# Later residual loads in the down product, an eighth slot for input tiles, and the gate's columns in quarters of the tokens

## The chip, the cores and the metric

The kernel runs on one core of one Trainium2 chip. The metric is the device time of one execution in microseconds (us), median of the runs; lower is better. The engines that matter are TensorE (PE in the profile, its weight loads PEld), VectorE (DVE), ScalarE (ACT), GpSimd (POOL) and SyncE (SP), whose queue issues nearly all DMA transfers.

## The reference

One layer on 1024 tokens of width 1024, all in float32:

```python
h = _rmsnorm(x, mix_norm_gain[l])
proj = h @ w_in[l]                                   # 1024 -> 3232 columns
y_rwkv = _rwkv7_mixer(proj[..., :RWKV_COLS], ...)    # 8 heads, gated delta rule; gate columns gd
o = _dilated_attention(q, k, v)                      # 8 heads, three dilations
x = x + jnp.concatenate([y_rwkv, y_attn], axis=-1) @ w_out[l]
h = _rmsnorm(x, ffn_norm_gain[l])
gate, val = jnp.split(h @ w_ffn_up[l], 2, axis=-1)   # 2 x 2816 columns
gate = _causal_dwconv(gate, ffn_conv_w[l], ffn_conv_b[l])
x = x + (jax.nn.silu(gate) * val) @ w_ffn_down[l]    # 2816 -> 1024
return _rmsnorm(x, final_norm_gain)
```

## The kernel before, in words

Every large product is made of two halves per operand: an upper half (the value rounded to the matmul's format, names with `hi` or `h`) and a lower half (value minus upper half, `lo` or `l`). A product is three matmuls: upper by upper, lower by upper, upper by lower (lines 475 to 477, 1752 to 1754). So each tile that is loaded costs a cast for the upper half (mostly ScalarE) and a subtraction for the lower one (VectorE or GpSimd, `lower`, line 301).

Order is written out by a planner, `Plan`: each operation has the engines that may do it with a cost, a rank, and the operations it comes after. `run` takes the operation that can start first by these costs, and the lowest rank among equals. The result is a fixed list of instructions for each engine. An engine works its list in order: an instruction that waits holds back all that is behind it, on SP too. A slot of a ring (`ring(name, n, ...)`) is given to a new tile when the tile n places earlier has been read by all its users. The operations named in `after` order the plan alone; in the program an instruction waits for data and for memory.

**Start (lines 404 to 574).** Eight tiles of x (128 tokens each, `x_0` to `x_7`) are loaded, two for each of four turns. `norm_turn` squares each (ScalarE, line 370, scratch `jk_n`), takes the reciprocal root (GpSimd), scales the tile (VectorE, line 376), transposes it in eight pieces (TensorE, line 386, into `pt_n`), and writes the upper and lower half of the transposed input, `hT_hi` (line 292 or 294) and `hT_lo` (line 395). Then `in_proj` multiplies by column blocks of w_in: `wa` (64 columns, twice), `gd` (the gate's 96 columns), then `k`, `r`, `v` and the attention's. Each block sums 512 tokens in one bank (`pb_wa`, `pb_gd`), first tokens 0 to 511, then the others. With `cut=2` the first 512 tokens are worked in two quarters of 256, so that they can begin when two turns are done. The banks come from a ring of two, so the second half of `wa` waits until the first has been read (`zwa`, and `carry_wa`, line 504). Small loads follow the input: `cst2`, `lwr` and `glr`, whose casts are `lwh` and `gl`. `grow_d` (line 337) writes 1024 gains of `par` to DRAM as a row, for the second norm far later.

**Down product (lines 1671 to 1772).** The 2816 rows of w_down are 22 factors of 128. Factor f needs a tile of the activation (`ra`, loaded from `act_d`) and one of the weights (`rw`), each split into four halves by `operand`. The steps (`groups`) hold one factor, one, and then three each. In a step the sums `pd` of eight token tiles by two column halves are formed in a ring of six banks and added to `dx` (line 1760; the first step copies instead, line 286 or 288). `residual` loads the layer's input `x1_d` into `dxs` and adds it to `dx` (line 1697) in steps three to six; `final` does the last norm in the last step. The load of a residual has a rank of its own and depended on `x1_stored` alone.

Of the kernel before, what the change touches and what calls it, by code (L numbers as in the profile page):

```python
# [18 lines left out]
P = 128  # L19
S = 1024  # L20
D = 1024
KD = D // P
# [9 lines left out]
GCOLS = 96  # L32
# [172 lines left out]
def planned_layer(ctx: ExitStack, tc: tile.TileContext, a, out):  # L205
    nc = tc.nc
# [13 lines left out]
    def ring(tag, n, shape, pool, dtype=F32):  # L220
        plan.ring(tag, n)
        if pool.space == PSUM:
            plan.banks.add(tag)

        def new(name):
            return plan.buf(tag, lambda: pool.tile(shape, dtype, tag=tag, name=name, bufs=n))

        return new
# [49 lines left out]
    def pool(us):  # L278
        return {POOL: us}
# [4 lines left out]
    def copy(eng, out, in_):  # L284
        if eng == ACT:
            nc.scalar.copy(out, in_)
        else:
            nc.vector.tensor_copy(out, in_)  # L288
# [10 lines left out]
    def lower(eng, lo, t, hi):  # L299

        either_of(eng).tensor_tensor(lo, t, f32(hi), ALU.subtract)  # L301
# [25 lines left out]
    def derived():  # L327
# [6 lines left out]
    g_ = _off["ffng"]  # L334
    grow_out = plan.op(
        {SP: 0.5},
        lambda: nc.sync.dma_start(out=grow_d.rearrange("o (k p) -> p (o k)", p=P), in_=par[:, g_ : g_ + KD]), -150, [par_in],
        lag=1.0,
    )
    par_in = plan.op({DVE: 0.5}, derived, -270, [par_in])  # L340
# [76 lines left out]
    scmask, bones = pc_[:, 0:256], pc_[:, 256:384]  # L417
    h_in = []
    with tc.tile_pool(name="xp", bufs=1) as xp:
        x_n, jk_n = ring("x", 7, [P, D], xp), ring("xjk", 1, [P, D], xp)  # L420
        for g in range(4):
            src = []
            for i in (2 * g, 2 * g + 1):
# [14 lines left out]
        def in_proj(cols, name, R, evacuate, after=None, Rw=None, twice=False, cut=1):  # L438

            raw, hi, lo = w_n(f"wr_{name}"), h_n(f"wh_{name}"), wl_n(f"wl_{name}")
            at, ins, Rw = 0, [], R if Rw is None else Rw
            for c0, n in cols:
                ins.append(
                    load(
                        raw, lambda at=at, n=n: raw.t[:, :, at : at + n],
                        lambda c0=c0, n=n: w_in[:, c0 : c0 + n].rearrange("(k p) c -> p k c", p=P), 1.46 * max(n, 128) / P, Rw,
                        [chain.get("w")],
                    )  # L450
                )
                at += n
            r, m = at, at * (1 + twice)

            def wide():
                return raw.t[:, :, None, :r].broadcast_to([P, KD, 2, r]) if twice else raw.t[:, :, :r]

            def parted(t):
                return t[:, :, :m].rearrange("p k (x c) -> p k x c", c=r) if twice else t[:, :, :m]

            Rw = max(Rw, -279.5)
            o = chain["w"] = plan.op(COPY, lambda eng: copy(eng, parted(hi.t), wide()), Rw, ins, [raw, hi, lo])
            o2 = plan.op(
                pool(2.3), lambda: lower(POOL, parted(lo.t), wide(), parted(hi.t)), Rw, [o], [raw, hi, lo]
            )
            outs = []
            for n in range(2):
                acc = acc_n(f"pb_{name}_{n}")
                d, c = None, 1 if n else cut
                for q, k in product(range(c), range(KD)):  # L470
                    w = 512 // c
                    ts_, cs = slice(n * 512 + q * w, n * 512 + (q + 1) * w), slice(q * w, (q + 1) * w)

                    def step(k=k, acc=acc, ts_=ts_, cs=cs):
                        nc.tensor.matmul(acc.t[:m, cs], hi.t[:, k, :m], hT_hi[k][:, ts_], start=(k == 0), stop=False)  # L475
                        nc.tensor.matmul(acc.t[:m, cs], hi.t[:, k, :m], hT_lo[k][:, ts_], start=False, stop=False)  # L476
                        nc.tensor.matmul(acc.t[:m, cs], lo.t[:, k, :m], hT_hi[k][:, ts_], start=False, stop=(k == KD - 1))  # L477

                    quarters = range(ts_.start // 256, ts_.stop // 256)
                    d = plan.op(  # L480
                        pe(0.69 / c), step, R, [o, o2, d, after, *(x for g in quarters for x in h_in[g][k])], [hi, lo, acc]
                    )
                outs.append(evacuate(n, acc, m, d))
            return outs

        def shift_mix(sh, dst, R, name, bufs=()):

            carry = st.tile([P, 1], F32, name=f"carry_{name}", bufs=1)

            def evacuate(n, acc, m, d):  # L490
                mu = par[:m, _off["sh_r"] + sh : _off["sh_r"] + sh + 1]
                c0 = n * 512

                def shifted():
                    t = dst()
                    nc.vector.scalar_tensor_tensor(
                        t[:m, c0 + 1 : c0 + 512], acc.t[:m, 0:511], mu, t[:m, c0 + 1 : c0 + 512], ALU.mult, ALU.add
                    )
                    if n:
                        nc.vector.scalar_tensor_tensor(  # L500
                            t[:m, 512:513], carry[:m], mu, t[:m, 512:513], ALU.mult, ALU.add
                        )
                    else:
                        nc.vector.tensor_copy(carry[:m], acc.t[:m, 511:512])

                o = plan.op(
                    {ACT: 0.57, DVE: 0.66},
                    lambda eng: scaled(eng, dst()[:m, c0 : c0 + 512], acc.t[:m], omm[:m, sh : sh + 1]), R, [d, par_in],
                    [acc, *bufs],
                )  # L510
                return plan.op({DVE: 0.79}, shifted, R, [o], [acc, *bufs])

            return evacuate
# [27 lines left out]
        lw_in = plan.op(LOW, lambda eng: lower(eng, flat(lwl), lwr.t, flat(lwh)), -184, [o], [lwr])  # L541

        zg = tmp_n("zg")
        z_in = in_proj([(1600, GCOLS)], "gd", -198, shift_mix(13, lambda: zg.t, -198, "gd", [zg]), None, -288.5)
        gr = slice(0, GCOLS)
        xg = pa_.tile([P, 2, S], F32R, name="xg")
        gl = pa_.tile([P, 2, RW], F32R, name="gl")
# [1136 lines left out]
    def down(acts, early, dp, pacc):  # L1684
# [4 lines left out]
        acc_n = ring("dacc", 6, [P, 512], pacc)  # L1689
        xr = [xr_n(f"dx{i}") for i in range(8)]  # L1690
        xsum = {i: [[], []] for i in range(8)}

        def residual(i, R):
            xs = jk_n(f"dxs{i}")
            o = load(xs, lambda: xs.t, lambda: x1_d[i], 1.46, R - 2, [x1_stored[i]])
            o = plan.op(
                {DVE: 1.22}, lambda: nc.vector.tensor_add(xr[i].t, xr[i].t, xs.t), R, [o, *xsum[i][0], *xsum[i][1]], [xs, xr[i]]
            )
            xsum[i] = [[o], [o]]
# [37 lines left out]
        for gi, fs in enumerate(groups):  # L1737
            R = 601 + 2 * gi
            ops = [operand(f, R, acts, raw_n, [(dh_n, dl_n)] * 2) if f else early for f in fs]
            if gi == 1:  # L1740
                fg_in = plan.op({SP: 0.5}, lambda: nc.sync.dma_start(out=fg, in_=a["fgain"].broadcast_to([P, D])), 990, lag=1.5)
            for i in range(8):
                ts_ = slice((i % 4) * P, (i % 4) * P + P)
                for n in range(2):
                    sl = slice(n * 512, (n + 1) * 512)
                    pd = acc_n(f"pd{gi}_{i}_{n}")
                    d = None
                    for j, o4 in enumerate(ops):
                        (ah, al, a_in), (wh, wl, w_in_) = o4[i // 4], o4[2 + n]

                        def step(j=j, ah=ah, al=al, wh=wh, wl=wl, ts_=ts_, pd=pd, n_=len(ops)):
                            nc.tensor.matmul(pd.t, ah.t[:, ts_], wh.t, start=(j == 0), stop=False)  # L1752
                            nc.tensor.matmul(pd.t, al.t[:, ts_], wh.t, start=False, stop=False)  # L1753
                            nc.tensor.matmul(pd.t, ah.t[:, ts_], wl.t, start=False, stop=(j == n_ - 1))  # L1754

                        d = plan.op(pe(0.7), step, R, [*a_in, *w_in_, d], [pd, ah, al, wh, wl])
                    if gi:
                        o = plan.op(
                            {DVE: 0.69},
                            lambda i=i, sl=sl, pd=pd: nc.vector.tensor_add(xr[i].t[:, sl], xr[i].t[:, sl], pd.t), R,  # L1760
                            [d, *xsum[i][n]], [pd, xr[i]],
                        )
                    else:
                        o = plan.op(
                            {ACT: 0.52, DVE: 0.62}, lambda eng, i=i, sl=sl, pd=pd: copy(eng, xr[i].t[:, sl], pd.t), R, [d],
                            [pd, xr[i]],
                        )
                    xsum[i][n] = [o]
                if gi in (2, 3, 4, 5) and i // 2 == gi - 2:
                    residual(i, R)  # L1770
                if gi == len(groups) - 1:
                    final(i, R)
# [142 lines left out]
```

## Time and profile before

| what | us |
|---|---|
| median of 3 runs (lowest, highest) | 1426.93 (1420.82, 1427.86) |
| the profiled execution | 1429.69 |
| its span, first to last instruction | 1427.5 |
| TensorE busy in the span | 1365.1 |
| VectorE, ScalarE, GpSimd busy | 999.3, 554.4, 340.8 |
| mean granted TensorE clock | 0.985 |

The profile is of one execution. A timeline row gives the start, the time, the engine, the line, the operation with out<-in and a count, and in brackets how long the engine was idle before it and what ended that. Times count from the first instruction. A granted clock of 1.00 is 2.4 GHz, of 0.50 it is 1.2 GHz; a value between is a mean over a stretch.

### The profile page before, as it was taken

To read this page: it belongs to the slowest core of one execution; us is meant where nothing else is said; L and a number is where in the kernel's file an instruction comes from. 1 tells how busy PE (TensorE), PEld (TensorE's weight loads), DVE (VectorE), ACT (ScalarE), POOL (GpSimd) and SP (SyncE) were. 2 spreads that over 40 slices of the span, in tenths; PEclk is the share of its full clock that TensorE was granted. 3 is DMA by queue.
4 is the path that set the end of the run, shared out by engine and by line. 5 is a ranking of instruction groups with operands and counts; after the bars stand their busy time and mean duration, and the time that the engine had idled before them with its cause. 6 is when DMAs were issued, how large, how long until landed. Compare 5 with 4: busy or idle time off the path is not lost.

```text
span 1427.5 us, 21004 instructions
## 1 busy us (share of the span) xinstructions
PE 1365.1 (96%) x7872; PEld 1129.4 (79%) x7872; DVE 999.3 (70%) x2020; ACT 554.4 (39%) x957; POOL 340.8 (24%) x366
## 2 busy tenths in 40 slices
PE   5999999999999889999989999999999999999997
PEld 4788887787788777888767888888888887888886
DVE  5566663867878378988589777777777757565547
ACT  5433332133222368776245434433333434222213
POOL 4223223143453357652231000000000005111101
PEclk9999999999999989999999999999999999999999
DMA  6143437545654446522743222222222237322203
GB/s 183 45 135 119 144 111 255 155 119 161 169 148 110 105 121 188 168 85 89 247 142 102 89 89 75 74 89 86 77 89 89 78 131 248 118 89 89 89 30 118
DMA packets 172565, 173.02 MB, mean 121 GB/s; under 512 B 39632, under 2 KB 142416, under 8 KB 171440
## 3 DMA queue, kind: packets, MB, share of 16 engines
q1 hardware_dynamic: 172320, 171.16, 39.4%
q8 instruction: 62, 1.02, 0.3%
q10 hardware_dynamic: 144, 0.52, 0.1%
q14 instruction: 39, 0.32, 0.1%
HBM read 119.22 MB, written 52.43 MB: 120 GB/s over the span
## 4 chain that ended last, share of the span: by engine, by line
PE 76%; DVE 11%; DMA 7%; ACT 1%; issue 1%; POOL 1%; SPq 1%; DVEq 0%; POOLq 0%; ACTq 0%
PE c L1554 29%; PE pd L1754 5%; PE pd L1752 5%; PE pd L1753 5%; PE po L1268 2%; PE pb_at L475 2%; DVE it L888 2%; PE po L1402 2%; PE po L1403 2%; PE po L1401 2%; PE ppt L1238 1%; DVE mp L894 1%; PE pb_at L477 1%; PE pb_at L476 1%; DMA mk<-md 1%
## 5 line engine op out<-in xcount | busy, mean ns | idle before, releaser
L301 POOL TENSOR_TENSOR wl<-rw,wh 128x512 fp32r<-128x512 f32 x22 | 32.8, 1496 | 558.0 <-ACT wh L1439 544.4
L1760 DVE TENSOR_TENSOR dx<-dx,pd 128x512 f32<-128x512 f32 x128 | 85.9, 684 | 86.4 <-PE pd L1754 85.8
L1754 PE MATMUL pd<-wl,ah 128*128 128x512 f32 x352 | 138.4, 393 | 2.8 <-POOL wl L301 2.8
L1752 PE MATMUL pd<-wh,ah 128*128 128x512 f32 x352 | 138.1, 392 | 0.2 <-DVE dx L288 0.2
L1753 PE MATMUL pd<-wh,al 128*128 128x512 f32 x352 | 138.1, 392 | 0.1
L1625 DVE TENSOR_TENSOR uval<-uval,c 128x512 f32<-128x512 f32 x67 | 45.9, 685 | 62.5 <-PE c L1554 62.3
L475 PE MATMUL pb_at<-hT_hi,wh_at 128*128 128x512 f32 x192 | 82.5, 430 | 0.0
L1754 PEld LDWEIGHTS pd<-wl,ah 128*128 128x128 f32 x352 | 66.7, 190 | 17.2 <-POOL wl L301 3.2
L1752 PEld LDWEIGHTS pd<-wh,ah 128*128 128x128 f32 x352 | 66.8, 190 | 14.6 <-DVE dx L288 0.6
L1753 PEld LDWEIGHTS pd<-wh,al 128*128 128x128 f32 x352 | 66.7, 189 | 14.6 <-POOL al L301 0.5
L477 PE MATMUL pb_at<-hT_hi,wl_at 128*128 128x512 f32 x192 | 76.3, 397 | 0.0
L476 PE MATMUL pb_at<-hT_lo,wh_at 128*128 128x512 f32 x192 | 76.2, 397 | 0.0
L1656 DVE SCALAR_TENSOR_TENSOR uga<-ug,par,uga 128x1023 f32<-128x1023 f32 (+1 forms) x44 | 56.4, 1281 | 15.8 <-ACT uga L1650 15.8
L888 DVE TENSOR_TENSOR it<-mk,mp 128x60 f32<-128x60 f32 (+19 forms) x240 | 64.0, 284 | 3.3
L894 DVE TENSOR_TENSOR mp<-mp,it 128x60 f32<-128x60 f32 (+20 forms) x240 | 54.5, 244 | 3.4
L1554 PE MATMUL c<-T,s1h 128*128 128x512 f32 x176 | 55.0, 393 | 1.0 <-DVE T L1498 1.0
L1554 PE MATMUL c<-B,a11h 128*128 128x512 f32 x176 | 54.9, 392 | 0.7 <-DVE B L1498 0.5
L1554 PE MATMUL c<-B,a12h 128*128 128x512 f32 x176 | 54.7, 392 | 0.7 <-ACT uval L1629 0.7
L1554 PE MATMUL c<-T,a22h 128*128 128x512 f32 x176 | 54.8, 393 | 0.0
L1554 PE MATMUL c<-B,s4h 128*128 128x512 f32 x176 | 54.8, 393 | 0.0
L1554 PE MATMUL c<-T,s3h 128*128 128x512 f32 x176 | 54.8, 393 | 0.0
L1554 PE MATMUL c<-T,s2h 128*128 128x512 f32 x176 | 54.8, 393 | 0.0
(335 smaller groups left out, 3722.0 us busy)
## 6 DMA issues: line engine op xcount, KB each, us to landing
rg<-in_w_up SPq DMA_DIRECT2D x22, 512.0 KB
rv<-in_w_up SPq DMA_DIRECT2D x22, 512.0 KB
ra<-act_d SPq DMA_DIRECT2D x22, 512.0 KB
rw<-in_w_down SPq DMA_DIRECT2D x22, 512.0 KB
act_d<-uga SPq DMA_DIRECT2D x21, 512.0 KB
x<-in_x SPq DMA_DIRECT2D x16, 512.0 KB
wr_at<-in_w_in SPq DMA_DIRECT2D x12, 512.0 KB
qkv_d<-spl SPq DMA_DIRECT2D x24, 256.0 KB
```

The lines of the kernel that those rows point to most:

```text
L475: nc.tensor.matmul(acc.t[:m, cs], hi.t[:, k, :m], hT_hi[k][:, ts_], start=(k == 0), stop=False)
L476: nc.tensor.matmul(acc.t[:m, cs], hi.t[:, k, :m], hT_lo[k][:, ts_], start=False, stop=False)
L477: nc.tensor.matmul(acc.t[:m, cs], lo.t[:, k, :m], hT_hi[k][:, ts_], start=False, stop=(k == KD - 1))
L888: nc.vector.tensor_tensor(t3(), mk.t[:, k : k + 1, k + 1 :].broadcast_to([P, r, n]), mp.t[:, 0:r, k : k + 1].broadcast_to([P, r, n]), ALU. ...
L894: nc.vector.tensor_tensor(mp.t[:, 0:r, k + 1 :], mp.t[:, 0:r, k + 1 :], t3(), ALU.add)
L1554: nc.tensor.matmul(bank.t, w.t[:, js], m, start=start and j == 0 and s, stop=j == 3 and w is lo, skip_group_check=True,)
L1625: {DVE: 0.69}, lambda: nc.vector.tensor_tensor(half_of(*out_), half_of(*x_), four(bank), ALU.add), R, after,
L1656: lambda x=x: nc.vector.scalar_tensor_tensor(ga.t[:, x:], g.t[:, : S - x], pc(f"cw{2 - x}", f), ga.t[:, x:], ALU.mult, ALU.add),
L1752: nc.tensor.matmul(pd.t, ah.t[:, ts_], wh.t, start=(j == 0), stop=False)
L1753: nc.tensor.matmul(pd.t, al.t[:, ts_], wh.t, start=False, stop=False)
L1754: nc.tensor.matmul(pd.t, ah.t[:, ts_], wl.t, start=False, stop=(j == n_ - 1))
L1760: lambda i=i, sl=sl, pd=pd: nc.vector.tensor_add(xr[i].t[:, sl], xr[i].t[:, sl], pd.t), R,
```

## The change

Four edits. The residual loads get a second condition in the plan, the first sum of the second down step (`begun[1]`). The input tiles get eight slots for seven, their scratch two for one. `gd` is worked with `cut=2`, and the lower halves of blocks with `cut` over 1 may be made by VectorE as well as by GpSimd. The rank of `grow_d` goes from -150 to 60.

```diff
--- before.py
+++ after.py
@@ -334,7 +334,7 @@
     g_ = _off["ffng"]
     grow_out = plan.op(
         {SP: 0.5},
-        lambda: nc.sync.dma_start(out=grow_d.rearrange("o (k p) -> p (o k)", p=P), in_=par[:, g_ : g_ + KD]), -150, [par_in],
+        lambda: nc.sync.dma_start(out=grow_d.rearrange("o (k p) -> p (o k)", p=P), in_=par[:, g_ : g_ + KD]), 60, [par_in],
         lag=1.0,
     )
     par_in = plan.op({DVE: 0.5}, derived, -270, [par_in])
@@ -417,7 +417,7 @@
     scmask, bones = pc_[:, 0:256], pc_[:, 256:384]
     h_in = []
     with tc.tile_pool(name="xp", bufs=1) as xp:
-        x_n, jk_n = ring("x", 7, [P, D], xp), ring("xjk", 1, [P, D], xp)
+        x_n, jk_n = ring("x", 8, [P, D], xp), ring("xjk", 2, [P, D], xp)
         for g in range(4):
             src = []
             for i in (2 * g, 2 * g + 1):
@@ -460,8 +460,9 @@
 
             Rw = max(Rw, -279.5)
             o = chain["w"] = plan.op(COPY, lambda eng: copy(eng, parted(hi.t), wide()), Rw, ins, [raw, hi, lo])
+            how = LOW if cut > 1 else pool(2.3)
             o2 = plan.op(
-                pool(2.3), lambda: lower(POOL, parted(lo.t), wide(), parted(hi.t)), Rw, [o], [raw, hi, lo]
+                how, lambda *eng: lower(*(eng or (POOL,)), parted(lo.t), wide(), parted(hi.t)), Rw, [o], [raw, hi, lo]
             )
             outs = []
             for n in range(2):
@@ -541,7 +542,7 @@
         lw_in = plan.op(LOW, lambda eng: lower(eng, flat(lwl), lwr.t, flat(lwh)), -184, [o], [lwr])
 
         zg = tmp_n("zg")
-        z_in = in_proj([(1600, GCOLS)], "gd", -198, shift_mix(13, lambda: zg.t, -198, "gd", [zg]), None, -288.5)
+        z_in = in_proj([(1600, GCOLS)], "gd", -198, shift_mix(13, lambda: zg.t, -198, "gd", [zg]), None, -288.5, False, 2)
         gr = slice(0, GCOLS)
         xg = pa_.tile([P, 2, S], F32R, name="xg")
         gl = pa_.tile([P, 2, RW], F32R, name="gl")
@@ -1689,10 +1690,11 @@
         acc_n = ring("dacc", 6, [P, 512], pacc)
         xr = [xr_n(f"dx{i}") for i in range(8)]
         xsum = {i: [[], []] for i in range(8)}
+        begun = {}
 
         def residual(i, R):
             xs = jk_n(f"dxs{i}")
-            o = load(xs, lambda: xs.t, lambda: x1_d[i], 1.46, R - 2, [x1_stored[i]])
+            o = load(xs, lambda: xs.t, lambda: x1_d[i], 1.46, R - 2, [x1_stored[i], begun[1]])
             o = plan.op(
                 {DVE: 1.22}, lambda: nc.vector.tensor_add(xr[i].t, xr[i].t, xs.t), R, [o, *xsum[i][0], *xsum[i][1]], [xs, xr[i]]
             )
@@ -1766,6 +1768,7 @@
                             [pd, xr[i]],
                         )
                     xsum[i][n] = [o]
+                    begun.setdefault(gi, o)
                 if gi in (2, 3, 4, 5) and i // 2 == gi - 2:
                     residual(i, R)
                 if gi == len(groups) - 1:
```

The first place is SP's order at the start: `x_7` is the last input tile, `wr_gd` the gate's columns. Before:

```order
L304 DMA x_5_160<-in_x 128x1024
L304 DMA x_6_162<-in_x 128x1024
L304 DMA wr_gd_175<-in_w_in 128x8x96
L337 DMA grow_d_85<-par_69 128x8x1
L304 DMA x_7_235<-in_x 128x1024
L308 DMA cst2_117<-in_consts2 128x384
L304 DMA lwr_310<-in_wa_lora 128x1024
```

And now:

```order
L304 DMA x_5_160<-in_x 128x1024
L304 DMA x_6_162<-in_x 128x1024
L304 DMA x_7_166<-in_x 128x1024
L304 DMA wr_gd_177<-in_w_in 128x8x96
L337 DMA grow_d_85<-par_69 128x8x1
L308 DMA cst2_117<-in_consts2 128x384
L304 DMA lwr_274<-in_wa_lora 128x1024
```

The tile moved ahead of `wr_gd` and `grow_d`, the rest stands as it stood, and `grow_d` kept its place between `wr_gd` and `cst2`.

The second place is ScalarE's order at the start: `jk_n1_3_1` is the square of the last input tile, `pt_n1_1_*` and `pt_n1_2_*` are the transposes of the second and third turn. Before:

```order
L292 ACTIVATE hT_hi4_99<-pt_n1_1_4_286,par_69 128x256
L292 ACTIVATE hT_hi5_100<-pt_n1_1_5_292,par_69 128x256
L292 ACTIVATE hT_hi6_101<-pt_n1_1_6_302,par_69 128x256
L370 ACTIVATE jk_n1_3_1_323,ss_n1_3_1_135<-x_7_235 128x1024
L292 ACTIVATE hT_hi7_102<-pt_n1_1_7_312,par_69 128x256
L286 CAST lwh_139<-lwr_310 128x1024
L286 CAST gl_143<-glr_320 96x512
L292 ACTIVATE hT_hi1_96<-pt_n1_2_1_363,par_69 128x256
```

And now:

```order
L370 ACTIVATE jk_n1_3_1_290,ss_n1_3_1_135<-x_7_166 128x1024
L286 CAST wh_gd_315<-wr_gd_177 128x8x96
L292 ACTIVATE hT_hi4_99<-pt_n1_1_4_292,par_69 128x256
L292 ACTIVATE hT_hi5_100<-pt_n1_1_5_295,par_69 128x256
L292 ACTIVATE hT_hi6_101<-pt_n1_1_6_303,par_69 128x256
L292 ACTIVATE hT_hi7_102<-pt_n1_1_7_311,par_69 128x256
L286 CAST lwh_139<-lwr_274 128x1024
L286 CAST gl_143<-glr_284 96x512
L292 ACTIVATE hT_hi0_95<-pt_n1_2_0_365,par_69 128x256
L292 ACTIVATE hT_hi1_96<-pt_n1_2_1_368,par_69 128x256
```

The square of the last tile moved ahead of the upper halves of the second turn; the casts `lwh` and `gl` still stand between the second turn and the third.

The third place is SP's order at the begin of the down product (`ra` and `rw` are the loads of a factor, `dxs` those of the residual, `fg` the last norm's gain). Before:

```order
L304 DMA rw1_11199<-in_w_down 128x1024
L304 DMA dxs0_11201<-x1_d_83 128x1024
L304 DMA dxs1_11203<-x1_d_83 128x1024
L304 DMA ra2_11205<-act_d_84 128x1024
L304 DMA rw2_11207<-in_w_down 128x1024
L304 DMA dxs2_11209<-x1_d_83 128x1024
L304 DMA dxs3_11211<-x1_d_83 128x1024
L304 DMA dxs4_11213<-x1_d_83 128x1024
L304 DMA dxs5_11215<-x1_d_83 128x1024
L1741 DMA fg_11180<-in_fgain 128x1024
L304 DMA ra3_11286<-act_d_84 128x1024
L304 DMA rw3_11320<-in_w_down 128x1024
```

And now:

```order
L304 DMA rw1_11223<-in_w_down 128x1024
L304 DMA ra2_11225<-act_d_84 128x1024
L304 DMA rw2_11227<-in_w_down 128x1024
L1743 DMA fg_11204<-in_fgain 128x1024
L304 DMA ra3_11298<-act_d_84 128x1024
L304 DMA rw3_11332<-in_w_down 128x1024
L304 DMA ra4_11355<-act_d_84 128x1024
L304 DMA dxs0_11376<-x1_d_83 128x1024
L304 DMA dxs1_11383<-x1_d_83 128x1024
L304 DMA rw4_11389<-in_w_down 128x1024
L304 DMA dxs2_11398<-x1_d_83 128x1024
L304 DMA dxs3_11405<-x1_d_83 128x1024
```

The residual loads moved behind the loads of the second factor, `fg`, and those of the third and most of the fourth.

## Rows read from the trace of the kernel before

**Rows 1.** the page's first part, busy time, share and count of each engine

```profile
PE 1365.1 (96%) x7872; PEld 1129.4 (79%) x7872; DVE 999.3 (70%) x2020; ACT 554.4 (39%) x957; POOL 340.8 (24%) x366
```

**Rows 2.** waits of TensorE, whole span: total us, times, longest us

```profile
PE pb_wa L475 <- ACT hT_hi L292: 5.0, 1, 5.0
...
PE pd L1754 <- POOL wl L301: 2.8, 1, 2.8
...
PE pb_wa L475 <- DVE carry_wa L504: 1.4, 1, 1.4
```

**Rows 3.** timeline of SP's issues at the start

```profile
5.97 0.43 SPq L304 DMA_DIRECT2D wr_gd<-in_w_in  x1
10.24 0.38 SPq L337 DMA_DIRECT2D grow_d<-par  x1
14.98 0.35 SPq L304 DMA_DIRECT2D x<-in_x  x1
...
15.86 0.42 SPq L304 DMA_DIRECT2D lwr<-in_wa_lora  x1
```

**Rows 4.** DMA traffic of 0 to 40 us, in slices of one us

```profile
GB/s 0 61 270 352 385 264 351 397 394 377 410 410 416 289 162 2 0 0 61 41 33 33 16 66 262 353 394 278 279 116 51 0 0 0 0 0 0 0 0 0
```

**Rows 5.** timeline of ScalarE at the start

```profile
26.88 1.06 ACT L370 ACTIVATE jk_n<-x 128x1024 f32<-128x1024 f32 x1 [6.18 <-DMA x<-in_x]
...
29.02 1.05 ACT L286 CAST lwh<-lwr 128x1024 fp32r<-128x1024 f32 x1 [0.63 <-DMA lwr<-in_wa_lora]
29.97 0.61 ACT L286 CAST gl<-glr 96x512 fp32r<-96x512 f32 x1
31.93 2.05 ACT L292 ACTIVATE hT_hi<-pt_n,par 128x256 fp32r<-128x256 f32 x5 [1.34 <-PE pt_n L386]
```

**Rows 6.** timeline of VectorE, third and fourth turn

```profile
34.68 4.00 DVE L395 SCALAR_TENSOR_TENSOR hT_lo<-pt_n,par,hT_hi 128x256 fp32r<-128x256 f32 x10
...
42.00 0.14 DVE L504 COPY carry_wa<-pb_wa 128x1 f32<-128x1 f32 x1
```

**Rows 7.** timeline of TensorE, matmuls of 256 columns and the second half of wa

```profile
22.26 0.28 PE L475 MATMUL pb_wa<-hT_hi,wh_wa 128*128 128x256 f32 x1
22.38 0.28 PE L476 MATMUL pb_wa<-hT_lo,wh_wa 128*128 128x256 f32 x1
...
42.29 0.47 PE L475 MATMUL pb_wa<-hT_hi,wh_wa 128*128 128x512 f32 x1 [1.38 <-DVE carry_wa L504]
```

**Rows 8.** windows: stretch, its length, busy by engine, PEclk, DMA share, GB/s

```profile
28.00:32.00 4.00, 3.55 (x12) 2.82 (x13) 3.57 (x4) 2.03 (x5) 2.59 (x3) 0.50 0.46 112
32.00:42.00 10.00, 8.18 (x46) 5.74 (x44) 10.00 (x21) 6.76 (x16) 2.38 (x4) 0.97 0.00 1
```

**Rows 9.** windows of TensorE alone, around the stop in the down product

```profile
1184.40:1197.10 12.70, 12.70 (x57) 1.00 0.81 291
1197.10:1206.90 9.80, 6.90 (x17) 0.65 0.75 248
1206.90:1216.70 9.80, 9.80 (x44) 1.00 0.65 227
```

**Rows 10.** timeline of SP in the down product

```profile
1172.01 9.74 SPq L304 DMA_DIRECT2D dxs<-x_d  x4
...
1182.64 0.32 SPq L304 DMA_DIRECT2D ra<-act_d  x1
```

**Rows 11.** timeline of VectorE there

```profile
1180.56 0.69 DVE L288 COPY dx<-pd 128x512 f32<-128x512 f32 x1 [2.79 <-DMA act_d<-uga]
```

**Rows 12.** timeline of ScalarE there

```profile
1190.53 1.15 ACT L1439 CAST ah<-ra 128x512 fp32r<-128x512 f32 x2 [3.85 <-DMA ra<-act_d]
```

**Rows 13.** timeline of GpSimd there

```profile
1191.22 2.56 POOL L301 TENSOR_TENSOR al<-ra,ah 128x512 fp32r<-128x512 f32 x2 [2.81 <-PE pd L1754]
...
1199.18 1.71 POOL L301 TENSOR_TENSOR wl<-rw,wh 128x512 fp32r<-128x512 f32 x1
```

## The prediction

> **What bounds the kernel now.** I read the page first: TensorE is busy 1365.1 of 1427.5 us [rows 1], so no other engine is worth anything unless it stops TensorE. Next the waits of TensorE over the whole span: the list is short, and two of its entries lie where the change is made. One is pb_wa (line 475), 5.0 us for an upper half of the normed input, with 1.4 more for carry_wa a little later; the other is pd (line 1754), 2.8 us for the lower half of a weight tile that GpSimd makes [rows 2]. Everything between is relative: no other instruction changes its place, so what the start gives is handed on to the end, and so is what the down product gives.
>
> At the start the chain is: ScalarE sits 6.18 us before the square of the last input tile and goes on at 26.88 [rows 5]. That load was issued at 14.98, since seven slots hold eight tiles and the first had to be transposed first [rows 3]. The queue then moves almost nothing: 2, 0, 0 and 61 GB/s in the microseconds from 15, then 41, 33, 33, 16, and from 24 on about 260 to 390 [rows 4]. What stands ahead of the tile there is grow_d, issued at 10.24 [rows 3], 1024 elements of four bytes written to DRAM.
>
> In the down product I read three stretches of equal kind: 57 matmuls in 12.70 us before 1197.1, 17 in 9.80 after it, 44 in the next 9.80 [rows 9]. At 0.223 each the 17 are worth 3.8 us; 6.0 us are lost: 2.8 in the full stop [rows 2], the other 3.2 by a granted clock of 0.65 in the mean (1.00 on both sides), which is 1.2 instead of 2.4 GHz for part of it. Backwards from the stop: GpSimd makes the late slice at 1199.18, after a row of subtractions that began at 1191.22 [rows 13], which began when ScalarE had its cast at 1190.53 after 3.85 us of waiting for ra [rows 12], whose load was issued at 1182.64, behind four residual loads on SP [rows 10].
>
> **The change part by part, the down product.** The six residual loads (512 KB each) go behind fg and most of the loads of factors 2, 3 and 4. SP's order shows ra2 and rw2 straight after rw1, then fg, ra3, rw3, ra4, two residual loads, rw4, four more. ra3 then waits only for its slot, the subtraction al1_1 on VectorE, which ran right after a copy dx that had waited 2.79 us for a store of act_d to land [rows 11]. In the changed program that copy no longer carries the wait, since its tile lies elsewhere. So ra3 is issued about 2 us earlier, at 1180.5, into an empty queue instead of behind four transfers. Its cast came 7.9 us after its issue with five transfers in line (1.6 each); alone I take 3 to 4 us, 1184.5 at the latest. ScalarE's own work before this cast ended at 1190.53 - 3.85 = 1186.7 [rows 12], so the load is no longer what is late.
>
> Late next is GpSimd. It was idle for 2.81 us before 1191.22, so its previous subtraction ended at 1188.4 [rows 13]; with the copy's wait gone I put that at 1187.5. Seven subtractions took 9.7 us (1191.22 to 1199.18 + 1.71); at the undisturbed 1.28 of the first pair they take 9.0. So the slice is ready at 1196.5 to 1197.2, or 1198.1 without the 0.9. rw4 has two residual loads in front; issued near 1187.5 behind ra4 and these, 4 x 1.6 us lands it near 1193, ahead of its turn on GpSimd at 1195. TensorE wants the slice at 1197.1. So 0 to 1 us of stop remains and no long one: of the 6.0 us I take back 5.9, with 5.0 and 6.0 as its ends where the mechanism holds. The residual loads are needed by adds that follow the third step's sums, near 1199 at the earliest, and should be down by then; the next step's factors have until 1197 + 33 us.
>
> **The start.** With an eighth slot the last tile is issued after its neighbour, before wr_gd and grow_d. It lands near 15, and its 6.18 us on ScalarE are gone. But behind its cast ScalarE's order holds lwh and gl, casts of lwr and glr, and both loads still stand behind grow_d; the upper halves of the third turn come after them. In the trace the first cast already waits for its load, at 29.02, and gl ends at 30.58 [rows 5]. So the wait changes its name. How early lwr lands is not shown; ends: the tile moved ahead delays grow_d by 512 KB at about 400 GB/s, 1.3 us, and leaves the queue behind it, 1.3 us less, which gives 29.0 again; no credit for the second gives 30.3; if the 184 KB that trickled from 18 to 23 [rows 4] now belong to lwr and grow_d ends no later, 26.5. I take 28.4, nearest to the row as it is.
>
> From there: lwh and gl 1.56 us [rows 5]; one upper half, 0.41 as five take 2.05 [rows 5]; then the chain of 16 lower halves, one upper and zwa to the end of carry_wa, which took 7.5 us (34.68 to 42.14) [rows 6]; 0.15 to TensorE: 9.6 us. TensorE adds something: the gate's first 512 tokens are now two quarters, 48 matmuls of 256 columns, 0.12 each [rows 7], for 24 of 0.22: 0.3 us in all. 21 of them stand behind the last transposes of the fourth turn, 2.5 us at full clock, 5.0 at half. The granted clock was 0.50 from 28 to 32, after the idle stretch, and 0.97 from 32 to 42 [rows 8]. TensorE will idle again, so I add 1.1 us (ends 0 and 3.4). pb_wa's second half then starts at 28.5 + 1.56 + 0.41 + 7.5 + 0.15 + 1.1 = 39.2, against 42.29 [rows 7]: 3.1 us. Ends: 6.1 (26.5, no clock loss) and -1.1 (30.3, 3.4).
>
> Edits at nothing: the lower halves of wa and gd move from GpSimd to VectorE, some 2 us of VectorE, hidden under the wait for lwr; without that cover they would cost their 2 us. The second jk slot lets squares overlap, hidden likewise. The new rank of grow_d moves nothing: it stands at the same place, between wr_gd and cst2, so this part doesn't do what it says.
>
> Sum: 5.9 + 3.1 = 9.0 us. Profiled execution: 1427.5 span, 1429.69 in all, so 1420.7. It lay 2.8 above the median of 1426.93; from the median the forecast is 1417.9.
>
> **Rivals.** (1) The start gives nearly nothing: lwr lands at 29.5 to 30.3 and the clock stays low through the narrow matmuls. For it: the empty slices behind grow_d, and lwr's place behind it; against it: fewer bytes in between. 0 to 1 us there, 6.4 in all: 1420.5. The Trainium skill (DMA: Bandwidth & Descriptors, Queues, rings and completion order) says that a transfer's completion increment lands only after every earlier write of the same DMA engine; the tile that waited behind grow_d agrees (issued 14.98, seen at 26.88), and by this rule lwr can't come before grow_d is done, which is this rival.
>
> (2) The down product's stop stays: VectorE's work slows GpSimd, as in the 1.71 of the last subtraction [rows 13]. Seven of these are 12.0, the slice comes at 1199.5, 2.4 us late, and the lower clock then costs about what it does now, 3.2. 6.0 - 5.6 + 3.1 = 3.5: 1423.4. Against it: four of the seven ran at 1.28.
>
> (3) lwr lands at 26.5 and the clock costs nothing: 6.1 + 5.9 = 12.0: 1414.9.
>
> (4) Slower: the residual add of the first tile stands on VectorE ahead of the third step's further sums. If its load came late, six banks of sums (each 9 x 0.223 = 2.0 us) fill by 1211, and TensorE stops with every later microsecond, plus 3.2 for the clock. It decides from a landing at 1217, and is slower by 0.5% from 1224: 1436 at 1226. Against it: the load is issued near 1186, and nothing in rows took longer than 11.9 us to land.
>
> **How the numbers follow.** Forecast 0.60 (own range 1415 to 1420.5), rival 1 0.17, rival 2 0.12, rival 3 0.07, rival 4 0.04. The range of 1412.5 to 1423.5 takes in rivals 1, 2 and 3. Half a per cent, 7.1 us, is about what a measurement of this kernel tells from no change; the line is at 1419.8. Faster: 0.55 of the forecast's share, 0.07 of rival 3, 0.05 of rivals 1 and 2: 0.67. Slower 0.04, the rest 0.29.
>
> **What would show it.** Right: ScalarE's long wait at the start is before lwh, for lwr, ending near 28.4, and the one before the square is gone; pb_wa's second half starts near 39; no wait of TensorE for wl at line 1756 and a granted clock of 1.00 from the second to the third down step; ra3's load issued about 2 us earlier against the step's start. Wrong: TensorE stops again within the first nine matmuls of the third step (GpSimd or rw4), a wait for dxs on VectorE, or lwh cast before 26.

## The result and the profile after

| what | before | changed |
|---|---|---|
| median of 20 runs each (lowest, highest) | 1424.81 us (1419.87, 1429.54) | 1415.93 us (1410.81, 1426.86) |
| ratio of the two | | 0.994 (95% interval 0.9926 to 0.9954) |
| the profiled execution, its span | 1429.69, 1427.5 | 1420.59, 1418.8 |

The changed kernel is 8.9 us faster (7 to 11), where 9.0 was forecast. Two later comparisons gave ratios of 0.9948 (0.9928 to 0.9969) and 0.9953 (0.9937 to 0.997), 7.4 and 6.7 us. The sum was right; by the average of the traces below, of its terms one was too small (the start), one too large (the down product), and one was missing (the middle, which takes some of the gain back).

The page's first part, after, to [rows 1]: TensorE's busy time is what it was, though the change added 24 matmuls and took none.

```profile
PE 1364.7 (96%) x7896; PEld 1132.7 (80%) x7896; DVE 989.7 (70%) x2023; ACT 554.5 (39%) x957; POOL 334.7 (24%) x363
```

The waits of TensorE, whole span, after, to [rows 2] (total us, times, longest). The 5.0 of pb_wa for hT_hi and the 2.8 of pd for wl have no row any more. The transposes pt_n now wait more for VectorE (3.9 instead of 1.1), and 0.5 is new.

```profile
PE pt_n L386 <- DVE hT_lo L395: 3.9, 3, 2.4
...
PE pb_gd L478 <- DVE wl_gd L301: 0.5, 1, 0.5
```

**Start.** SP's issues, the DMA traffic in slices of one us, and ScalarE, after, to [rows 3 to 5]:

```profile
7.75 0.38 SPq L304 DMA_DIRECT2D wr_gd<-in_w_in  x1
10.68 1.34 SPq L337 DMA_DIRECT2D grow_d<-par  x1
...
15.61 0.43 SPq L304 DMA_DIRECT2D lwr<-in_wa_lora  x1
```

```profile
GB/s 0 61 262 361 391 265 364 398 388 395 410 410 410 414 315 203 187 106 20 41 37 41 20 53 29 80 337 237 248 49 0 0 0 0 0 0 0 0 0 0
```

```profile
20.66 0.83 ACT L286 CAST wh_gd<-wr_gd 128x768 fp32r<-128x768 f32 x1 [2.36 <-DMA wr_gd<-in_w_in]
...
27.72 1.04 ACT L286 CAST lwh<-lwr 128x1024 fp32r<-128x1024 f32 x1 [4.75 <-DMA lwr<-in_wa_lora]
28.67 0.61 ACT L286 CAST gl<-glr 96x512 fp32r<-96x512 f32 x1
```

The trickle behind grow_d is still there (20 to 53 GB/s from 18 to 24, full rate from 26), and ScalarE's long wait is now the one before lwh. TensorE and its clock, after, to [rows 7, 8] (the windows give TensorE alone: length, busy, clock, DMA share, GB/s):

```profile
30.23 0.83 PE L386 MATMUL pt_n<-cst,x 128*128 128x128 f32 x4 [2.45 <-DVE hT_lo L395]
...
38.55 0.47 PE L476 MATMUL pb_wa<-hT_hi,wh_wa 128*128 128x512 f32 x1 [0.29 <-DVE carry_wa L505]
```

```profile
28.00:31.70 3.70, 1.48 (x12) 1.00 0.33 80
31.70:35.20 3.50, 3.50 (x19) 0.51 0.00 0
```

TensorE waits 2.45 us until 30.23, works on at full clock until 31.7, then 3.5 us at half clock, and begins the second half of wa at 38.55 instead of 42.29.

**Down product.** The same three stretches as [rows 9], 2.1 us earlier as the first sum is (1171.16 for 1173.24):

```profile
1182.30:1195.00 12.70, 12.70 (x57) 1.00 0.93 356
1195.00:1204.80 9.80, 9.80 (x45) 1.00 0.94 355
1204.80:1214.60 9.80, 9.80 (x45) 1.00 0.57 200
```

No stop, and full clock throughout. Behind it, SP, ScalarE, GpSimd and VectorE, after, to [rows 10 to 13]:

```profile
1178.18 0.33 SPq L304 DMA_DIRECT2D ra<-act_d  x1
...
1183.54 0.91 SPq L304 DMA_DIRECT2D dxs<-x_d  x2
```

```profile
1183.56 1.14 ACT L1440 CAST ah<-ra 128x512 fp32r<-128x512 f32 x2
...
1192.13 1.15 ACT L1440 CAST wh<-rw 128x512 fp32r<-128x512 f32 x2 [4.29 <-DMA rw<-in_w_down]
```

```profile
1192.83 1.30 POOL L301 TENSOR_TENSOR wl<-rw,wh 128x512 fp32r<-128x512 f32 x1 [0.23 <-ACT wh L1440]
```

```profile
1198.25 1.22 DVE L1699 TENSOR_TENSOR dx<-dx,dxs 128x1024 f32<-128x1024 f32 x1
```

ra3 goes out 7.0 us after the first sum's begin instead of 9.4, and its cast has no wait. The slice that stopped TensorE is ready at 1194.13; it is wanted near 1195.0 (23.86 after the first sum, as 1197.1 was before).

### The profile page after: what moved, and what is told of

It reads as the page before. It is cut to its first block, busy times and chain, and to the rows that moved or that the text cites. A ratio compares the mean times of both kernels' runs of the same rounds, so it can differ in the third digit from the quotient of the medians.

```text
span 1418.8 us, 21048 instructions
## 1 busy us (share of the span) xinstructions
PE 1364.7 (96%) x7896; PEld 1132.7 (80%) x7896; DVE 989.7 (70%) x2023; ACT 554.5 (39%) x957; POOL 334.7 (24%) x363
## 4 chain that ended last, share of the span: by engine, by line
PE 80%; DVE 9%; DMA 6%; SPq 2%; issue 1%; ACT 1%; POOL 1%; DVEq 0%; POOLq 0%; ACTq 0%
PE c L1555 29%; PE pd L1756 5%; PE pd L1755 5%; PE pd L1754 5%; PE po L1269 2%; PE pb_at L476 2%; PE ppt L1239 2%; PE po L1402 2%; PE po L1403 2%; PE po L1404 2%; SPq L304 2%; PE pb_at L478 1%; PE pb_at L477 1%; DVE it L889 1%; DVE mp L895 1%
## 5 line engine op out<-in xcount | busy, mean ns | idle before, releaser
L301 POOL TENSOR_TENSOR wl<-rw,wh 128x512 fp32r<-128x512 f32 x21 | 29.2, 1391 | 552.7 <-PE pd L1755 429.5
L889 DVE TENSOR_TENSOR it<-mk,mp 128x60 f32<-128x60 f32 (+19 forms) x240 | 59.2, 264 | 3.3
```

Source lines behind the costliest of these rows:

```text
L889: nc.vector.tensor_tensor(t3(), mk.t[:, k : k + 1, k + 1 :].broadcast_to([P, r, n]), mp.t[:, 0:r, k : k + 1].broadcast_to([P, r, n]), ALU. ...
```

## The experiments

Each kernel was timed against the kernel before on its own chip. Where the time went is read from the traces in three parts: the start up to the second half of wa, the middle up to the first pd, and the down product from there to its last matmul. In brackets stands how much of a part the trace's record of the granted clock shows at 1.2 GHz. Where TensorE sets the pace such time costs half of itself (in the down product of the kernel before, matmuls of 512 columns begin 0.43 us apart in it and 0.23 us at full clock); where something else does, it costs less, so the fourth column takes off rather too much.

| kernel | start | middle | middle less half of its bracket | down product | ratio to before (95%) |
|---|---|---|---|---|---|
| before | 42.29 (6.8) | 1130.95 (23.9) | 1119.0 | 246.13 (6.8) | |
| before_again | 41.83 (6.8) | 1129.09 (27.3) | 1115.4 | 243.92 (3.4) | 1.0004 (0.9989, 1.0019) |
| resid_only | 42.04 (6.8) | 1132.57 (27.3) | 1118.9 | 239.48 (0) | 0.9974 (0.9962, 0.9986) |
| dx_first | 42.20 (6.8) | 1130.70 (27.3) | 1117.1 | 248.54 (6.8) | 1.0037 (1.0023, 1.0051) |
| grow_only | 36.56 (0) | 1131.49 (30.7) | 1116.1 | 243.95 (3.4) | 0.997 (0.9958, 0.9981) |
| grow_and_resid | 36.58 (0) | 1128.49 (23.9) | 1116.5 | 239.49 (0) | 0.9939 (0.9916, 0.9961) |
| changed | 38.55 (3.4) | 1132.61 (27.3) | 1119.0 | 239.46 (0) | 0.994 (0.9926, 0.9954) |
| after_again | 38.94 (3.4) | 1131.10 (23.9) | 1119.2 | 239.48 (0) | 0.9948 (0.9928, 0.9969) |
| after_third | 37.20 (0) | 1133.06 (23.9) | 1121.1 | 239.48 (0) | 0.9953 (0.9937, 0.997) |
| start_only | 37.28 (3.4) | 1130.25 (23.9) | 1118.3 | 243.87 (3.4) | 0.9981 (0.9967, 0.9995) |
| old_memory | 36.33 (0) | 1134.66 (30.7) | 1119.3 | 239.54 (0) | 0.9957 (0.994, 0.9975) |
| grow_late | 35.82 (0) | 1132.81 (27.3) | 1119.2 | 239.49 (0) | 0.9946 (0.9927, 0.9965) |
| grow_later | 35.89 (0) | 1130.78 (20.5) | 1120.5 | 239.48 (0) | 0.9928 (0.9905, 0.995) |
| grow_later_2 | 35.72 (0) | 1132.73 (23.9) | 1120.8 | 239.49 (0) | 0.9946 (0.9928, 0.9964) |

The six rows ahead of the changed kernel have seven slots, the others eight.

**The parts alone: start_only and resid_only.** start_only is the changed kernel without `begun[1]` in the list of `residual`; resid_only is the kernel before with that condition.

```
-            o = load(xs, ..., [x1_stored[i], begun[1]])   # start_only
+            o = load(xs, ..., [x1_stored[i]])
```

> All of the change but the condition on the residual loads. Theory: the start and the down product are two gains that add up. TensorE begins the second half of wa near 38.6 as in the changed kernel (42.29 before), so 3.1 to 3.7 us sooner; the down product keeps its stop of 2.8 us and its low clock. 1421 us. Rival (what the start gives is given back by stretches of lower clock in the middle): the same early begin, but 0 to 2 us in the end, 1423 to 1425 us.

> The kernel before with nothing but the condition on the residual loads. Theory: the stop of 2.8 us before wl goes and the clock stays at 1.00 there; 5.9 us by the prediction, 6.7 by the trace of the changed kernel: 1418 to 1419 us. Rival (the two parts need each other, or the down product's gain is lost to another wait): under 4 us, over 1421 us.

Measured: start_only 1422.19 beside 1425.66 us, 2.7 us less by the ratio (0.7 to 4.7); resid_only 1421.87, 3.7 less (2.0 to 5.4). start_only lies between its theory (1421) and its rival (1423 to 1425). The two add to 6.4, which neither 8.9 nor 6.7 us contradicts. In both, the other part is untouched: resid_only starts wa at 42.04, start_only keeps its stop:

```profile
PE pd L1756 <- POOL wl L301: 2.6, 1, 2.6
```

resid_only lies in its rival's band by time (under 4 us), though its down product has no stop and full clock and takes 239.48 us, as in the changed kernel. The next run shows why the 5.9 were too many. start_only's second half of wa starts at 37.28, 4.8 us sooner than on average in the four traces that start like the kernel before (42.1), where its theory had 38.6; its time shows less.

**The kernel before once more.**

> The kernel before, unchanged, run against itself for the size of what a comparison can show, and for a second trace. Theory (the down product's loss is the stop plus as much of the stretch of lower clock as falls after it, which differs between executions): a stop of 2.5 to 3.0 us before wl again, with 3.4 or 6.8 us of lower clock behind it, so first sum to last matmul of the down product 243.9 to 246.1 us; ratio 1.000. Rival (the first trace's 246.1 us is what the kernel always takes): 246 us again.

Measured: 1427.39 beside 1426.9 us. Its trace, TensorE alone, around the stop:

```profile
1194.90:1204.60 9.70, 7.19 (x25) 0.82 0.77 253
```

The mean clock is 0.82 there, not 0.65: the stop is 2.5 us, and 3.4 us at half clock follow instead of 6.8. start_only and grow_only, which keep the stop, show 3.4 as well. So the down product gives 4.4 us in three of the four traces that have the stop, dx_first below left out (243.9 less 239.5), and 6.7 only in the one that the prediction was read from.

**Queue or memory: old_memory and dx_first.** In the kernel before, two things delayed the data of ra3: the residual loads ahead of it on SP, and the copy dx3, whose tile lay where a store of act_d still read. The change removed both, the second only because the scratch tiles are now made after the sums. Each was put back alone: old_memory is the changed kernel with one scratch tile made first, which gives the whole ring of six its memory ahead of the sums; dx_first is the kernel before with the sums made first.

```
         xr_n = ring("dx", 8, [P, D], dp)
+        dp.tile([P, D], F32, tag="djk", name="djk_", bufs=6)    # old_memory
```

```
         xr = [xr_n(f"dx{i}") for i in range(8)]
+        for x_ in xr:                                            # dx_first
+            x_.t = x_.make()
+            plan.used["dx"].append(x_)
```

> The changed kernel, but the six scratch tiles of the down product (dxs) get their memory ahead of the eight sums (dx), as before; so the copies dx0 and dx3 wait again for stores of act_d to land. The residual loads stay late. Theory (SP's queue was what made ra3 late): the copy waits 1 to 2 us, ra3 is issued that much later, and the slack of about 1 us that the last slice of the third step has takes most of it; TensorE stops for 0 to 1 us, 1416 to 1418 us. Rival (the copy's wait for the store was the cause): the stop near 2.8 us and the low clock return, 6 us more, 1422 us.

> The kernel before, but the eight sums dx get their memory ahead of the scratch tiles dxs, as in the changed kernel; the residual loads stay where they stood. So no copy waits for a store of act_d. Theory (SP's queue makes ra3 late): the copies run early, ra3 is still issued behind four residual loads, and the stop before wl stays, 2 to 4 us; 1424 to 1427 us. Rival (the copies' wait was the cause): the stop is gone, 1420 us.

old_memory: 1419.37 beside 1425.66 us, 6.1 less (3.6 to 8.6). The copy waits again, and ra3 is issued 8.6 us after the first sum instead of 7.0 (at 1179.58, the sum at 1170.99):

```profile
1177.66 0.69 DVE L288 COPY dx<-pd 128x512 f32<-128x512 f32 x1 [2.15 <-DMA act_d<-uga]
```

TensorE doesn't stop and the down product takes 239.54. The time is above the theory's 1416 to 1418. The clean partner of this trace is start_only: there too the scratch tiles come ahead of the sums, and the same copy waits as long (2.21 us); only the residual loads are early. ra3 is issued 8.7 us after the first sum there and 8.6 here, so the issue is the same. But its cast follows 7.6 us behind the issue in start_only, after a wait of 3.39 us, and at most 4.1 us behind it, without a wait, in old_memory (start_only first):

```profile
1183.78 1.14 ACT L1440 CAST ah<-ra 128x512 fp32r<-128x512 f32 x2 [3.39 <-DMA ra<-act_d]
```

```profile
1183.64 1.19 ACT L1440 CAST ah<-ra 128x512 fp32r<-128x512 f32 x2
```

(The first sums are at 1167.53 in start_only and 1170.99 in old_memory, the issues at 1176.19 and 1179.58.) start_only stops for 2.6 us and old_memory doesn't. What made ra3 late is thus the transfers ahead of it, and not the time of its issue. All nine traces with late residual loads are without the stop, and all five with early ones have it.

dx_first: 1432.69 beside 1426.9 us, slower by 5.3 (3.3 to 7.3), outside both its theory and its rival. No copy waits for a store, and TensorE stops more than before, its waits from 1196 to 1205:

```profile
1198.52 0.50 PE L1757 MATMUL pd<-wl,ah 128*128 128x512 f32 x1 [1.53 <-POOL wl L301]
...
1200.99 0.80 PE L1756 MATMUL pd<-wh,al 128*128 128x512 f32 x1 [1.23 <-POOL al L301]
1204.34 0.80 PE L1757 MATMUL pd<-wl,ah 128*128 128x512 f32 x1 [2.55 <-POOL wl L301]
```

But dx_first is no clean removal: with the sums made first, the tiles of the loads get other memory too, and rw1 waits for VectorE's last product of the activation; SP in dx_first:

```profile
1175.52 0.33 SPq L304 DMA_DIRECT2D rw<-in_w_down  x1
1175.94 0.90 SPq L304 DMA_DIRECT2D dxs<-x_d  x2
1176.93 0.74 SPq L304 DMA_DIRECT2D ra<-act_d  x1
```

In the kernel before, dxs went out from 1160.00 and this ra at 1171.06. So old_memory beside start_only settles that late residual loads remove the stop with the copy's wait left in place; whether taking away the wait alone would remove it, dx_first can't say, since it makes the loads later as well.

**The start: grow_d really moved.** grow_late and grow_later are the changed kernel with the write defined later in the plan, behind the load of glr, or behind the gate's second half, which puts it behind wr_r on SP.

```
-    grow_out = plan.op({SP: 0.5}, lambda: ..., 60, [par_in], lag=1.0)
+    par_there = par_in
...
+        grow_out = plan.op({SP: 0.5}, lambda: ..., 60, [par_there, o], lag=1.0)          # grow_late: o loads glr
+        grow_out = plan.op({SP: 0.5}, lambda: ..., 60, [par_there, z_in[1]], lag=1.0)    # grow_later
```

> The changed kernel with the write grow_d really moved, behind the loads of cst2, lwr and glr. Theory (its 1024 elements of four bytes hold back whatever stands behind them on the queue): lwr has landed by 18 us, the wait of 4.75 us before lwh is gone, most of the 2.36 us before wh_gd too, TensorE doesn't stop for 2.45 us near 28 and keeps its clock; second half of wa near 34 instead of 38.6, so 4 to 5 us less than the changed kernel: 1411 us. Rival (the loads lwr, cst2 and wr_gd are late by their own, or by the queue's order of issue): lwh stays near 27.7, under 1 us less, 1415 us. Rival 2: the write now holds back wr_k, TensorE waits for wh_k, and nothing is won: 1416 us.

> The changed kernel with the write grow_d moved further still, behind the loads of wr_k and wr_r, so that it is issued near 47 us. Theory (the write holds back transfers issued just ahead of it as well, as glr when it was issued 0.5 us earlier): no wait for lwr or glr on ScalarE, gl cast by 24 us instead of 25.5 and 28.7; the third turn is then held by VectorE and TensorE, so the second half of wa starts at 35 us, 0.5 to 1 us sooner than with the smaller move: 1414 us. Rival (glr is late for another reason): it is still cast at 25 us or later.

> The changed kernel, unchanged. Theory: second half of wa between 36.3 and 38.6 us, down product 239.5 us without a stop; the middle between them 1119 us plus half of its time at the lower clock (24 to 31 us in the traces so far); 1416 us. Rival (what the start gives is spent in the middle by later waits): a middle over 1120 us when the lower clock is taken off.

> The changed kernel, unchanged, to stand beside the next one on the same chip. Theory: as in its two traces, second half of wa at 38.5 to 39 us, down product 239.5 us, 8 to 9 us under the kernel before.

> The changed kernel with grow_d behind wr_r, a second time, beside the changed kernel itself. Theory: second half of wa near 35.9 us, 2.6 to 3.0 us sooner, and 2 to 4 us less in the end than the changed kernel, 10 to 12 us under the kernel before. Rival (the start's gain is given back in the middle): no measurable difference to the changed kernel.

Measured: grow_late 1418.14 beside 1425.66; after_again 1420.57 and grow_later 1416.83, both beside 1426.9; after_third 1418.76 and grow_later_2 1417.76, both beside 1426.04. ScalarE of grow_late and then of grow_later:

```profile
21.87 1.04 ACT L286 CAST lwh<-lwr 128x1024 fp32r<-128x1024 f32 x1
25.46 0.62 ACT L286 CAST gl<-glr 96x512 fp32r<-96x512 f32 x1 [2.56 <-DMA glr<-in_g_lora]
```

```profile
21.95 1.04 ACT L286 CAST lwh<-lwr 128x1024 fp32r<-128x1024 f32 x1
22.89 0.62 ACT L286 CAST gl<-glr 96x512 fp32r<-96x512 f32 x1
26.44 2.30 ACT L292 ACTIVATE hT_hi<-pt_n,par 128x256 fp32r<-128x256 f32 x6 [2.93 <-PE pt_n L382]
```

So the write holds back what stands behind it: with the small move lwr is no longer waited for. It also held glr, issued 0.47 us ahead of it (12.19 and 12.66): in the trace's DMA packets all 96 of glr (2048 bytes each) have ended by 19.35 us and the traffic is 8 GB/s in the microsecond from 19 and none in the next three, yet the cast of glr waits until 25.46. By this record its data had moved, and only the sign that it had landed was late. With the larger move the cast doesn't wait, and behind the write no load follows on SP until 60 us. The second half of wa starts at 35.7 to 35.9 either way, 0.4 to 3.2 us sooner than in the five traces that start like the changed kernel (36.33 to 38.94), because the third turn is then held by TensorE's transposes (the 2.93 above). That is less than the 4 to 5 us expected of grow_late; 34 was wrong. In time grow_later lies 1.0 to 2.9 us under the changed kernel beside it by the ratios, within the intervals: a gain there is not shown, nor one of grow_late. Other expectations were missed too: the second half of wa came at 38.94 in after_again (by 38.6 expected) and at 37.20 in after_third (38.5 to 39 expected), after_third gained 6.7 us where 8 to 9 were expected, and grow_later_2 gained 7.7 where 10 to 12 were, and 1.0 over the changed kernel where 2 to 4 were.

**The cheap version: grow_only and grow_and_resid.** grow_only is the kernel before with grow_d behind wr_r and nothing else; grow_and_resid has the condition on the residual loads as well. No eighth slot, no quarters.

> The kernel before, and only grow_d moved behind wr_r: still seven slots, one scratch, the gate's columns in one piece, residual loads early. Theory (the write was the one thing that held the start): x_7, issued near 15 as before, lands by 18 us, its square no longer waits 6 us, lwr and glr follow by 20 us; second half of wa near 37 us instead of 42, as much as the eighth slot and the quarters together gave; 4 to 5 us less than the kernel before, with the down product's stop unchanged. Rival (the late issue of x_7 at 15 us by itself was the cost): square after 22 us, second half of wa after 40 us.

> The kernel before with two of its moves only: grow_d behind wr_r, and the residual loads behind the second step's first sum. Seven slots, one scratch and the gate's columns in one piece, as before. Theory (the start was held by the write, the down product by the queue, and slots and quarters are not needed for either): second half of wa near 36.6 us, down product 239.5 us, no stop; the two gains add to 8 to 10 us, as much as the whole change or a little more: 1416 to 1418 us beside 1425 to 1427 of the kernel before. Rival (one of the two is given back in the middle): 1420 us or more.

grow_only: 1421.25 beside 1426.04, 4.3 us less (2.7 to 6.0). x_7 is issued at 15.30 as before, and its square runs without a wait, as do the casts behind it:

```profile
21.20 1.08 ACT L366 ACTIVATE jk_n<-x 128x1024 f32<-128x1024 f32 x1
22.25 0.49 ACT L292 ACTIVATE hT_hi<-pt_n,par 128x256 fp32r<-128x256 f32 x1
22.60 1.08 ACT L286 CAST lwh<-lwr 128x1024 fp32r<-128x1024 f32 x1
```

wa's second half starts at 36.56, as early as with the eighth slot and the quarters (36.33 to 38.94). grow_and_resid: 1417.18 beside 1424.72, ratio 0.9939 (0.9916 to 0.9961). Moving the write and the residual loads does what the whole change does.

## Why the prediction came out

- **Down product, 5.9 us: the mechanism right, the size read from one execution.** The stop is gone, clock 1.00, ra3 2.4 us earlier against the first sum (2 predicted; 1.6 to 1.9 against the other three traces with the stop). The term of 3.2 us for the lower clock is the one mis-sized: 1.7 in three of four traces (half of 3.4 us). Against its own trace the part gave 6.7; against the average of the four, 5.0. That execution was above its median for this among other reasons.
- **The reason for ra3's earlier issue** was given as the copy's lost wait. That is worth 1.6 us of issue time (old_memory), but no time of TensorE once the residual loads are out of the way; moving them is what removes the stop.
- **Late next: GpSimd.** Not quite. The last load, rw4, is: ScalarE waited 4.29 us for it, GpSimd 0.23 for the cast. It was forecast to land near 1193, which is 1190.9 after the shift, and it was cast at 1192.13. The slack was 0.9 us, so no stop.
- **Start, 3.1 us: 3.7 in the trace, 4.4 on average.** The mis-sized term is when lwr comes, of which the prediction said that it was not shown. lwr is cast at 27.72, at 28.49 and 27.61 in the other two traces of the changed kernel, and at 26.43 and 26.73 in start_only and old_memory, which start alike (28.4 predicted): grow_d moved back and the tile ahead of lwr moved away, as worked out. The chain behind this cast was right. Up to the second half of wa it takes 9.6 us in the two traces without lower clock (after_third and old_memory; 9.6 worked out) and 10.45 to 10.85 in the three with 3.4 us of it. So the lower clock cost 0.9 to 1.3 us where it came (1.1 predicted) and nothing elsewhere. Mean of the five traces 37.7, against 42.1 in the four that start like the kernel before.
- **"What the start gives is handed on": failed by 1.7 us.** The middle took 1132.61 instead of 1130.95, all of it lower clock: 27.3 us of it instead of 23.9. This differs between executions of one kernel (23.9 and 27.3 for before, too), so in this pair it can be scatter. But the middle as measured averages 1132.25 in the eight traces with eight slots and 1130.55 in the six with seven, and with half of the lower clock taken off 1119.7 and 1117.2. From 43 us up to the residual loads at its end every engine has the same instructions in the same order (the write aside, where it was moved); the cause of these 2 us is open.
- **Edits at nothing** nearly held: TensorE waits 0.5 us for wl_gd, and grow_d stands where it stood.
- **Rivals.** 1: lwr did come only when the trickle ended, but that came early enough to leave 3.7 us. The Trainium skill (DMA: Bandwidth & Descriptors, Queues, rings and completion order) orders a completion behind earlier writes of the same DMA engine; lwr in the changed kernel does not contradict it (issued at 15.61 behind grow_d, cast at 27.72), though its packets moved slowly as well; glr in grow_late, which was ahead of the write, lies outside what it says. 2: fell; GpSimd's pairs ran at 1.28. 3: its start came in old_memory (lwr cast at 26.73, no lower clock, second half of wa at 36.33), and after_third had no lower clock there either. 4: the residual add ran at 1198.25 without a wait.

The agreement of 9.0 with 8.9 is partly luck. In the two profiled executions the errors are +0.6 for the start, +0.8 for the down product and -1.7 for the middle. On average the parts are 4.4, 5.0 and -1.7, in all 7.7 us.

## What to carry to other kernels

When a load is late, look at what else is in the queue before giving it another buffer: one 4 KB write of four-byte elements cost the start 5.5 us (42.1 against 36.56 in grow_only), and moving it was worth as much as an extra slot and a finer split. That the size of the elements is what makes it dear, no run tests. A load that is not urgent belongs behind those that are, but check which memory its tile then gets, since in dx_first the order in which tiles were made cost 5.3 us by itself. A stop of TensorE is priced from several executions, as the clock behind it differs.

## What the hardware showed unexpectedly

- The 4 KB write grow_d kept transfers waiting for 7 to 8 us (18 to 25 us in the changed kernel), those issued behind it, and in grow_late the landing of one issued 0.47 us ahead. The write's own packets are not what lasts: in the changed kernel's trace some thousand packets of four bytes start between 15 and 18 us, and then, from 18 to 25 us, the 4096-byte packets of the loads behind take 1.4 us each in the mean instead of the 0.16 of 10 to 13 us.
- After one and the same stop of 2.5 to 2.8 us TensorE's clock was low for 3.4 or 6.8 us, which makes 1.7 or 3.4 us. In the middle it was low for 20.5 to 30.7 us of some 1130, which is up to 5 us between two executions.
- At the start, 3.4 us of low clock cost only 0.9 to 1.3 us.
